# Modulated projections of a diffusion layer: half of the shifts added after the first eight outputs

## The chip, the cores and the metric

The kernel runs on one core of a Trainium2 chip. The core has five engines with a queue each: TensorE (PE; its weight loads are listed as PEld), VectorE (DVE), ScalarE (ACT), GpSimd (POOL) and SyncE (SP, here for transfers only). Sixteen DMA engines move data between the chip's memory (HBM), SBUF and back; PE writes to PSUM. The metric is device time in microseconds (us) of one execution, as the median of the runs shown.

## The reference

One layer over 512 latent tokens x of width 2048, with 256 context tokens ctx. A condition vector c modulates the latent tokens, another, c_ctx, the context tokens. Cut to what the change touches:

```python
sc_ = silu(c); scc = silu(c_ctx)
mod_x = sc_ @ w_ada + b_ada            # w_ada: 2048 x (6 * 2048)
mod_c = scc @ w_ada + b_ada
sh1, s1, g1, sh2, s2, g2 = split(mod_x, 6); sh1c, s1c = first two of mod_c
h  = rmsnorm(x,   norm1_w) * (1 + s1)  + sh1
hc = rmsnorm(ctx, norm1_w) * (1 + s1c) + sh1c
p, pc = h @ w_in, hc @ w_in            # queries, keys, values of 8 heads; low-rank cq (384), ckv (256); k_rope (64)
# keys and queries get a rotary embedding (latent tokens alone), cq and ckv an RMSNorm
```

Differential attention and latent attention over context and latent tokens, the output projection and a gated MLP with a convolution follow; the change leaves them as they are. All numbers are float32. Since h is a sum of a scaled token and a shift that is the same for every token, h @ w_in is the scaled tokens' product plus one number for each output feature, shift @ w_in.

## The kernel before

**Layout.** Tokens lie along the free axis and features on the 128 partitions, in 16 tiles kt of 128 features. A projection's *feature* is a block of 128 output features; its weights come as two blocks of 512 KB (eight kt each, `wblock`, L87 and L90), and it is a sum over 16 kt. Every float32 factor is split into a high part (rounded by ACT, `wh`, `a2k`, `c2k`) and a low part (what is left, a subtraction on DVE, L81), and a product is three matmuls (`mm3`, L104 to L106): high by high, high by low, low by high. With 512 latent and 256 context tokens a feature is 96 matmuls. `a2k` tiles hold latent tokens (512 wide), `c2k` two context tiles of 256.

**The modulation.** c and c_ctx are loaded as rows, go through SiLU on ACT and are spread over 128 partitions by PE (L199), into `cb` and `ccb`. A modulation number is a dot product of 2048 terms. `scales(u)` makes the scales of the pair kt = 2u, 2u + 1 on PE: four loads of 512 KB (`adak`, four buffers), 32 narrow matmuls with c and c_ctx in two of 32 columns (`cpad`, L219), a copy, two matmuls with `sel` that add up four partial sums (L223), and `a1` on DVE (L235). `shifts(kt)` makes the shift: two halves of 512 KB on SP's queue (L244), and for even kt two custom sums on DVE a half (L251, one for c and one for c_ctx, 1024 wide); for odd kt 16 PE transposes (L258) and 32 narrow matmuls. The later modulations (second shift and scale, gate; 48 blocks of 1 MB) are `gemv`s: a load (L168, SP's queue, two buffers) and one custom sum on DVE (L171).

**The stages.** First, squares of the tokens on ACT (L276, L277), their sums over features on PE with a matrix of ones (L282, L284), and the reciprocal root (L157). Then for kt from 0 to 15: the modulation of the next pair, the scaled and shifted tokens (`h` on DVE, L330, high part on ACT, L332, low part on DVE, L333), and nine outputs at once in PSUM: five features of the latent tokens (two of ckv, the keys of heads 0 and 1, the query of head 0) and four of the context. After these come seven single features with context (keys of heads 2 to 7 and k_rope), with three `gemv`s each; three of cq with two each; V in two halves of eight blocks, with one or two `gemv`s a block; then the heads, whose scores are L482.

**What sets the order.** Each engine works its queue in order. The program is written as one sequence; a scheduler that reckons with costs of its own spreads it over the engines' queues ahead of the run, and puts instructions under `high_priority` early. A transfer whose buffer is not free waits at the head of its queue, and what stands behind it in the queue waits too. `reuse_waits="tile"` makes a pool's next user wait for the same tile's last reader alone. Only the MLP's end is written in an order by hand.

Of the kernel before, what the change touches and what calls it, by code (L numbers as in the profile page):

```python
# [9 lines left out]
F32 = mybir.dt.float32  # L10
# [7 lines left out]
P = 128  # L18
# [34 lines left out]
def layer_kernel(ctx: ExitStack, tc: tile.TileContext, small, rope, c_row, cc_row, x_t, ctx_t, ada, ada_k,  # L53
# [33 lines left out]
    def wblock(src, cols=1024, pool=None):  # L87
        pool, full = (pool, cols) if pool else (wp, 1024)
        raw = pool.tile([P, full], F32, tag="wr", name=nm("wr"), bufs=3 if full == 1024 else 2)
        nc.sync.dma_start(raw[:, :cols], src)  # L90
        hi = pool.tile([P, full], F32R, tag="wh", name=nm("wh"), bufs=3)
        lo = pool.tile([P, full], F32R, tag="wl", name=nm("wl"), bufs=3)
        split(hi[:, :cols], lo[:, :cols], raw[:, :cols])
        return hi, lo
# [15 lines left out]
    sm.tile([P, 88], F32, name="edge")  # L110
# [69 lines left out]
    hcp = tc.alloc_tile_pool(name="hcp", bufs=17, side="right")  # L180
# [3 lines left out]

    st = tc.alloc_tile_pool(name="st", bufs=1, reuse_waits="tile")

    cb = st.tile([P, D], F32, name="cb")
    ccb = st.tile([P, D], F32, name="ccb")  # L190
# [3 lines left out]
    for row, wide in ((c_row, cb), (cc_row, ccb)):  # L194
        nc.sync.dma_start(wide[0:1], row)
        sc.activation(wide[0:1], wide[0:1], AF.Silu)
        for j in range(0, D, 512):
            t = b_tile()
            pe.matmul(t, ones32[0:1], wide[0:1, j:j + 512], start=True, stop=True)  # L199
            ve.tensor_copy(wide[:, j:j + 512], t)  # L200
    exp_ln_tables()

# [6 lines left out]

    g0b = [b_tile() for _ in range(4)]  # L210
    acc = g0b[3]

    def products(src, n):


        for j in range(4):
            for c in range(4):
                kt = 4 * j + c
                pe.matmul(acc[32 * c:32 * c + 32, :n], cpad[:, kt], src(kt), start=j == 0, stop=j == 3)  # L219
        row = st.tile([P, 2 * P], F32, tag="row", name=nm("row"), bufs=1)[:, :n]  # L220
        sc.copy(row, acc[:, :n])
        for i in range(n // P):
            pe.matmul(acc[:, 2 * i:2 * i + 2], row[:, i * P:(i + 1) * P], sel, start=True, stop=True)  # L223

    def scales(u):

        ws = []
        for j in range(4):
            wk = st.tile([P, 4, 2 * P], F32, tag="adak", name=nm("adak"), bufs=4)
            nc.sync.dma_start(wk, ada_k[u, j // 2][:, (j % 2) * 4:(j % 2) * 4 + 4])  # L230
            ws.append(wk)
        products(lambda kt: ws[kt // 4][:, kt % 4], 2 * P)
        for i in range(2):
            kt = 2 * u + i
            ve.tensor_scalar(out=a1[:, 2 * kt:2 * kt + 2], in0=acc[:, 2 * i:2 * i + 2], scalar1=b1[:, kt:kt + 1],  # L235
                             scalar2=col("n1", kt), op0=ALU.add, op1=ALU.mult)

    def shifts(kt):


        ws = []
        for hf in range(2):
            w = st.tile([P, D // 2], F32, tag="ada", name=nm("ada"), bufs=5)
            nc.sync.dma_start(w, ada[kt][:, hf * D // 2:(hf + 1) * D // 2])  # L244
            ws.append(w)
        dst = [m[:, kt:kt + 1] for m in (modx, modc)]
        if kt % 2 == 0:
            for hf, w in enumerate(ws):
                for i, (vec, d) in enumerate(zip((cb, ccb), dst)):
# [5 lines left out]
        for q in range(4):  # L255
            for i in range(4):
                k = (q % 2) * 4 + i
                pe.transpose(acc[:, i * P:(i + 1) * P], ws[q // 2][:, k * P:(k + 1) * P], ident)  # L258
# [1015 lines left out]
```

## Time and profile before

| | |
|---|---|
| median of 3 runs (lowest, highest) | 2450.04 us (2447.59, 2454.52) |
| profiled execution | 2454.1 us, span 2451.9 us, mean granted clock 0.988 |
| PE busy | 2375.5 us, 97% of the span |
| DVE, ACT, POOL busy | 1726.3, 1102.5, 242.1 us |
| moved by DMA | 403.31 MB, mean 164 GB/s |
| queue of SP and ACT, queue of POOL | 350.87 MB, 49.30 MB |

The page's slices cut the span into 40 equal parts of 61.3 us; a digit is the busy share in tenths. A stretch of a table by stage has its length, the busy time and number of instructions of each engine, the clock that was granted to PE, the DMA share and GB/s. A group is a line of the program, engine, operation, output and inputs, shapes, the number of instructions, then the busy time, the mean ns of one, and the idle time of the engine ahead of them with what ended it. In the chain of waits each row is a start, a length, and the work or wait that held up what came after.

### The profile page before, as it was taken

Reading aid. Unit: us, or ns where it says so; the run is one execution under the profiler, and the core shown is the slowest. Engines: PE = TensorE matmul, PEld = TensorE weight load, DVE = VectorE, ACT = ScalarE, POOL = GpSimd, SP = SyncE. Lnnn points to the kernel's source line nnn. Section 1 sums busy time; section 2 is a strip of 40 time slices with the busy share of each in tenths; the row PEclk is TensorE's granted clock in tenths of the full one; section 3 lists DMA queues with packets and bytes.
Section 4 is the critical chain, followed back from the end, with each engine's and each line's share of the span. In section 5 each row is a group of like instructions: output and inputs, shape, how many; then the busy total and the mean of one; then the engine's idle time right before and its main releaser. Section 6 shows DMA issues by size and latency. Waiting matters only on the chain.

```text
span 2451.9 us, 32940 instructions
## 1 busy us (share of the span) xinstructions
PE 2375.5 (97%) x12788; PEld 1988.9 (81%) x12788; DVE 1726.3 (70%) x2272; ACT 1102.5 (45%) x1666; POOL 242.1 (10%) x270
## 2 busy tenths in 40 slices
PE   7999999999999999999999999999999999999997
PEld 3778887877777778888888888888888888888887
DVE  4668785388868877377666666666666666666667
ACT  4342121155545542244545454545454545454553
POOL 0000000122100003100111111111111111111113
PEclk8999999999999999999999999999999999999999
DMA  7868898554411149423555655555555555555572
GB/s 276 283 228 297 321 340 289 189 181 137 141 59 44 44 159 337 152 85 112 134 141 135 141 135 141 134 142 134 140 135 143 133 143 133 144 132 142 133 213 78
DMA packets 130706, 403.31 MB, mean 164 GB/s; under 512 B 14323, under 2 KB 25075, under 8 KB 122099
## 3 DMA queue, kind: packets, MB, share of 16 engines
q1 hardware_dynamic: 104118, 350.87, 43.4%
q0 software_dynamic: 25280, 49.30, 11.5%
q8 instruction: 100, 1.64, 0.3%
q10 hardware_dynamic: 1152, 1.05, 0.1%
q14 instruction: 56, 0.46, 0.1%
HBM read 331.68 MB, written 69.48 MB: 164 GB/s over the span
## 4 chain that ended last, share of the span: by engine, by line
PE 84%; DVE 8%; ACT 3%; DMA 3%; issue 1%; POOL 1%; SPq 0%; DVEq 0%; ACTq 0%; POOLq 0%
PE y L973 12%; PE b L105 10%; PE b L104 10%; PE b L106 10%; PE z L973 6%; PE y L975 6%; PE z L975 3%; PE s L104 3%; PE s L105 3%; PE s L106 3%; PE s L482 3%; PE x L973 2%; DMA ada<-in_ada 2%; PE x L975 1%; PE f L104 1%
## 5 line engine op out<-in xcount | busy, mean ns | idle before, releaser
L104 PE MATMUL b<-ah,wh 128*128 128x512 f32 (+1 forms) x672 | 259.1, 386 | 0.0
L105 PE MATMUL b<-al,wh 128*128 128x512 f32 (+1 forms) x672 | 259.0, 385 | 0.0
L106 PE MATMUL b<-ah,wl 128*128 128x512 f32 (+1 forms) x672 | 258.0, 384 | 0.0
L994 POOL DMA_DIRECT2D x_d<-xs x160 | 139.7, 1003 | 1166.4 <-ACT xs L993 1164.3
L949 DVE TENSOR_TENSOR wl<-wr,wh 128x1024 fp32r<-128x1024 f32 x126 | 153.8, 1221 | 128.7 <-ACT wh L943 128.7
L949 DVE TENSOR_TENSOR wl<-rb,wh 128x1024 fp32r<-128x1024 f32 x124 | 151.2, 1220 | 128.0 <-ACT wh L943 128.0
L80 ACT CAST wh<-wr 128x1024 fp32r<-128x1024 f32 (+3 forms) x118 | 115.9, 982 | 259.0 <-PE b L105 68.3
L943 ACT CAST wh<-wr 128x1024 fp32r<-128x1024 f32 x126 | 132.3, 1050 | 206.3 <-PE b L105 100.7
L943 ACT CAST wh<-rb 128x1024 fp32r<-128x1024 f32 x124 | 130.2, 1051 | 190.0 <-PE b L105 112.5
L949 DVE TENSOR_TENSOR wl<-ws,wh 128x1024 fp32r<-128x1024 f32 x123 | 150.1, 1221 | 88.8 <-ACT wh L943 88.8
L81 DVE TENSOR_TENSOR wl<-wr,wh 128x1024 fp32r<-128x1024 f32 (+3 forms) x118 | 137.3, 1164 | 89.4 <-ACT wh L80 89.0
L171 DVE CUSTOM_DVE_ANT_0 ada<-ada,cb,smt 128x2048 f32<-128x2048 f32 x64 | 151.6, 2369 | 62.4 <-DMA ada<-in_ada 62.1
L943 ACT CAST wh<-ws 128x1024 fp32r<-128x1024 f32 x123 | 128.3, 1043 | 137.0 <-PE b L105 45.2
L106 PEld LDWEIGHTS b<-ah,wl 128*128 128x128 f32 x672 | 126.3, 188 | 25.6
L104 PEld LDWEIGHTS b<-ah,wh 128*128 128x128 f32 x672 | 126.6, 188 | 22.9
L105 PEld LDWEIGHTS b<-al,wh 128*128 128x128 f32 x672 | 126.6, 188 | 22.0
L104 PE MATMUL b<-a2k,wh 128*128 128x512 f32 (+1 forms) x352 | 133.1, 380 | 6.6 <-ACT a2k L756 5.0
L106 PE MATMUL b<-a2k,wl 128*128 128x512 f32 (+1 forms) x352 | 132.5, 376 | 0.0
L973 PE MATMUL y<-b2k,wh 128*128 128x512 f32 x410 | 106.9, 390 | 0.0
L484 DVE TENSOR_REDUCE m<-s 128x1 f32<-128x768 f32 x96 | 90.5, 949 | 15.3 <-PE s L482 14.9
L993 ACT ACTIVATE xs<-b,modx 128x512 f32<-128x512 f32 x160 | 101.0, 680 | 0.5 <-PE y L973 0.3
L973 PEld LDWEIGHTS y<-b2k,wh 128*128 128x128 f32 x410 | 77.0, 188 | 17.1
(471 smaller groups left out, 5937.4 us busy)
## 6 DMA issues: line engine op xcount, KB each, us to landing
ada<-in_ada SPq DMA_DIRECT2D x64, 1024.0 KB, 6.8
rb<-in_w_up SPq DMA_DIRECT2D x123, 512.0 KB, 4.4
wr<-in_w_dn SPq DMA_DIRECT2D x84, 512.0 KB, 4.3
x_d<-xs POOLq DMA_DIRECT2D x160, 256.0 KB, 6.0
wr<-in_w_up SPq DMA_DIRECT2D x53, 512.0 KB, 4.2
wr<-in_w_f SPq DMA_DIRECT2D x34, 512.0 KB, 5.9
adak<-in_ada_k SPq DMA_DIRECT2D x32, 512.0 KB, 6.2
ada<-in_ada SPq DMA_DIRECT2D x32, 512.0 KB, 6.6
```

The costliest lines, as they stand in the source:

```text
L80: sc.copy(dst_h, src)
L81: ve.tensor_tensor(dst_l, src, dst_h.bitcast(F32), op=ALU.subtract)
L104: pe.matmul(out, st[0], mv[0], start=start, stop=False, **kw)
L105: pe.matmul(out, st[0], mv[1], start=False, stop=False, **kw)
L106: pe.matmul(out, st[1], mv[0], start=False, stop=stop, **kw)
L171: ve.tensor_tensor_reduce(out=junk, in0=w, in1=vec, op0=ALU.mult, op1=ALU.add, scale=1.0, scalar=col("b_ada", j), accum_out=dst[:, j:j + 1])
L943: sc.copy(hi, raw)
L949: ve.tensor_tensor(lo, raw, hi.bitcast(F32), op=ALU.subtract)
L973: pe.matmul(o, w[j][0], hs[j], start=start and j == 0, stop=False, skip_group_check=True)
L975: pe.matmul(o[:, h0], w[j][1], hs[j][:, h0], start=False, stop=j == 7, skip_group_check=True)
L993: sc.mul(x, po, modx[:, 80 + dt:81 + dt])
L994: gp.dma_start(x1_d[dt], x, accum_op=ALU.add)
```

## The change

- Tokens are loaded first. The condition rows come later, spread over 128 partitions by the load itself (1 MB each), and SiLU runs on all partitions; PE's broadcast is gone. `cb` stays in place for the whole projection part.
- All 16 shifts are sums on DVE, with halves loaded on POOL's queue, three buffers. PE's transposes and narrow matmuls for odd kt are gone. Three halves are issued ahead of a copy on POOL that waits for `ccb`.
- While the nine first outputs are made, only the shifts of kt 8 to 15 are computed and applied. kt 0 to 7 go in scaled but unshifted. The outputs are copied as they are, and kept (`keep`).
- The next three features (`EARLY`) are projected from the same half-shifted tokens and kept too, while shifts 0 to 7 are computed. Then `add_shift` puts these into the tokens: high and low part are added, shifted, and split again. The fourth feature takes its second half of kt first.
- `biases` makes what is missing from the eight outputs: the eight blocks of the first outputs and three first half blocks of weights are loaded again, raw, through the two raw buffers of the ring, and multiplied by the shifts in 40 narrow matmuls. `with_bias` adds it to the kept outputs, and their keys, query and norms are made after features 3, 4 and 5.
- `gemv`s: none with feature 3, two with 4 to 6, three with each of cq, three or two with V's blocks. Rings: raw weight blocks have two buffers instead of three up to the end of V; `adak` six instead of four.

```diff
-    for row, wide in ((c_row, cb), (cc_row, ccb)):
-        nc.sync.dma_start(wide[0:1], row)
-        sc.activation(wide[0:1], wide[0:1], AF.Silu)
-        for j in range(0, D, 512):
-            t = b_tile()
-            pe.matmul(t, ones32[0:1], wide[0:1, j:j + 512], start=True, stop=True)
-            ve.tensor_copy(wide[:, j:j + 512], t)
...
+        for hf in range(2):
+            w = sp_.tile([P, D // 2], F32, tag="ada", name=nm("ada"), bufs=3)
+            gp.dma_start(w, ada[kt][:, hf * D // 2:(hf + 1) * D // 2])
+            for i, (vec, d) in enumerate(zip((cb, ccb), dst)):
+                t = w if i else sp_.tile([P, D // 2], BF16, tag="junk", name=nm("junk"), bufs=1)
+                ve.tensor_tensor_reduce(out=t, in0=w, in1=vec[:, hf * D // 2:(hf + 1) * D // 2], op0=ALU.mult,
+                                        op1=ALU.add, scale=1.0, scalar=d if hf else col("b_ada", kt), accum_out=d)
...
     modulation(0)
+    for row, wide in ((c_row, cb), (cc_row, ccb)):
+        nc.sync.dma_start(wide, row.to_broadcast([P, D]))
+        sc.activation(wide, wide, AF.Silu)
+    gate = sm.tile([P, 1], F32, name="gate")
+    gp.tensor_copy(gate, ccb[:, 0:1])
...
     for kt in range(KT):
-        if kt % 2 == 0 and kt < KT - 2:
-            modulation(kt // 2 + 1)
+        if kt % 2 == 0:
+            if kt < KT - 2:
+                modulation(kt // 2 + 1)
+            shifts(KA + kt // 2)
...
+                if kt < KA:
+                    split(*hl, t)
+                else:
+                    shifted(*hl, t, m[:, kt:kt + 1])
...
+    def add_shift(kt):
+        for i, (hl, m, n_) in enumerate(((hx[kt], modx, T), (hc[kt], modc, C))):
+            t = rtmp()[:, :n_]
+            ve.tensor_tensor(t, hl[0].bitcast(F32), hl[1].bitcast(F32), op=ALU.add)
+            shifted(*hl, t, m[:, kt:kt + 1])
...
+        for kt in range(KA):
+            w = wraw(w_g0[kt], 640)
+            r = slice(32 * (kt % 4), 32 * (kt % 4) + 32)
+            pe.matmul(ac[0][r], spad[:, kt], w[:, :512], start=kt < 4, stop=kt >= KA - 4)
+            pe.matmul(ac[1][r, :P], spad[:, kt], w[:, 512:640], start=kt < 4, stop=kt >= KA - 4, skip_group_check=True)
+        for e in range(EARLY):
+            w = wraw(w_f[feats[e], 0])
...
+    for e in range(EARLY):
         lat, co = b_tile(), s_tile()
         feature(lat, co[:, :C])
+        for kt in (range(3), range(3, 6), range(6, 8))[e]:
+            shifts(kt)
+        keep(5 + e, lat, co[:, :C])
+    for kt in range(KA):
+        add_shift(kt)
+    sp_.release()
+    gvp = tc.alloc_tile_pool(name="gvp", bufs=1, side="right", reuse_waits="tile")
+    for f in range(EARLY, 7):
+        lat, co = b_tile(), s_tile()
+        feature(lat, co[:, :C], halves.get(f, (0, 1)))
         keys(k_d[f + 2] if f < 6 else kr_d, lat, co[:, :C])
-        next_gemv(kv, 3)
+        if f == EARLY:
+            biases()
...
+        next_gemv(gvp, 2 if f > EARLY else 0)
```

Three places show how the queues change. The first is DVE's queue ahead of the second pair's scales (`a_91`). Before, the shift of kt 1 came from PE, two short additions (L262) stood there, with the low parts of the first tokens:

```order
L262 TENSOR_SCALAR modx<-b_189,smt 128x1
L262 TENSOR_SCALAR modc<-b_189,smt 128x1
L333 SCALAR_TENSOR_TENSOR a2k_567<-h_568,modx,a2k_566 128x512
L333 SCALAR_TENSOR_TENSOR c2k_529<-h_568,modc,c2k_528 128x256
L235 TENSOR_SCALAR a_91<-b_189,b_92,smt 128x2 x2
L330 SCALAR_TENSOR_TENSOR h_704<-a2k_205,a_91,rinv 128x512
```

Now ten sums of shift halves (L248) stand there, of which the last six are these (each is followed by an entry of one column that writes the sum):

```order
L248 ISA ada_532,modc<-ada_532,ccb,smt 128x1024
L248 ISA modc 128x1
L248 ISA junk_539,modx<-ada_537,cb,modx 128x1024
L248 ISA modx 128x1
L248 ISA ada_537,modc<-ada_537,ccb,modc 128x1024
L248 ISA modc 128x1
L248 ISA junk_660,modx<-ada_658,cb,smt 128x1024
L248 ISA modx 128x1
L248 ISA ada_658,modc<-ada_658,ccb,smt 128x1024
L248 ISA modc 128x1
L237 TENSOR_SCALAR a_91<-b_220,b_92,smt 128x2 x2
L321 SCALAR_TENSOR_TENSOR h_546<-a2k_175,a_91,rinv 128x512
```

So the second pair's scales, which PE's sums give, are behind shift sums of later tiles that read `cb` and `ccb`.

The second place is DVE's queue in the middle of `add_shift`, which the program before doesn't have (L444 adds the parts, L303 makes the new low part, L174 is a `gemv`, L81 a weight block's low part):

```order
L444 TENSOR_TENSOR rt_1799<-a2k_544,a2k_545 128x512
L444 TENSOR_TENSOR rt_1803<-c2k_542,c2k_543 128x256
L174 ISA ada_2276,modx<-ada_2276,cb,smt 128x2048
L174 ISA modx 128x1
L81 TENSOR_TENSOR wl_1757<-wr_1754,wh_1756 128x1024
L303 SCALAR_TENSOR_TENSOR a2k_545<-rt_1799,modx,a2k_544 128x512
L303 SCALAR_TENSOR_TENSOR c2k_543<-rt_1803,modc,c2k_542 128x256
L444 TENSOR_TENSOR rt_1807<-a2k_580,a2k_581 128x512
L444 TENSOR_TENSOR rt_1811<-c2k_542,c2k_543 128x256
L174 ISA ada_2279,modx<-ada_2279,cb,smt 128x2048
```

Four `gemv`s and three low parts of weights stand among the additions ahead of the last one.

The third place is SP's queue at the raw blocks of `biases`. Before, a feature's blocks and the `gemv` loads alternated in twos:

```order
L389 DMA k_d_130<-kl_1929 128x768
L90 DMA wr_2043<-in_w_f 128x1024
L90 DMA wr_2049<-in_w_f 128x1024
L168 DMA ada_2069<-in_ada 128x2048
L168 DMA ada_2072<-in_ada 128x2048
L90 DMA wr_2176<-in_w_f 128x1024
L90 DMA wr_2182<-in_w_f 128x1024
```

Now:

```order
L89 DMA wr_1989<-in_w_g 128x640
L89 DMA wr_1993<-in_w_g 128x640
L171 DMA ada_2713<-in_ada 128x2048
L89 DMA wr_1997<-in_w_g 128x640
L89 DMA wr_2001<-in_w_g 128x640
L171 DMA ada_2716<-in_ada 128x2048
L89 DMA wr_2005<-in_w_g 128x640
L89 DMA wr_2009<-in_w_g 128x640
L171 DMA ada_2719<-in_ada 128x2048
L89 DMA wr_2013<-in_w_f 128x1024
L89 DMA wr_2023<-in_w_f 128x1024
```

Raw blocks, in twos, and 1 MB loads of `gemv`s stand in turns in one queue.

More of the change, by code (lines that the diff above doesn't have):

```diff
@@ L225, in scales @@
[L225 to L236, printed above, removed]
```

214 lines of the change are left out of this document (127 added, 87 removed).

## The prediction

> **What bounds the kernel now.** I read the page's slices first, then the chain of waits up to 620 us, then busy time by stage, and last the groups of instructions inside the stages that the change touches. Times are us from the span's start.
>
> ```profile
> PE   7999999999999999999999999999999999999997
> DVE  4668785388868877377666666666666666666667
> ```
>
> TensorE is nine tenths busy in every slice except the first and the last, so only time in which it idles, or works on something that can go, is to be had. The chain says what that is at the start:
>
> ```profile
> 7.16 14.02 PE b L199 x16
> 26.55 1.57 PE s L282 x4
> 28.83 1.57 PE s L282 x4
> 39.49 1.30 PE s L284 x4
> 47.62 1.54 DVE h L330 x3
> 52.37 1.22 PE s L104 x2
> 364.13 7.53 DMA ada<-in_ada
> 374.07 7.40 DMA ada<-in_ada
> ```
>
> The condition vector is broadcast for 14 us before the sums of squares can run (2.28 us for two token tiles), and the first projection matmul comes at 52.37. Far later, the V projection waits for the 1 MB loads of the modulation: one buffer of the two comes round every 9.9 us.
>
> ```profile
> 52.00:186.00 134.00, 129.34 (x1076) 98.68 (x1076) 89.72 (x174) 50.86 (x99) 0.00 (x0) 0.97 0.73 249
> 186.00:270.00 84.00, 83.26 (x470) 72.15 (x471) 70.61 (x98) 22.13 (x29) 0.00 (x0) 1.00 0.85 308
> 270.00:344.00 74.00, 74.00 (x369) 61.64 (x368) 60.49 (x67) 18.02 (x24) 0.00 (x0) 1.00 0.90 338
> 344.00:411.00 67.00, 66.40 (x293) 54.38 (x291) 46.34 (x47) 11.82 (x14) 0.00 (x0) 1.00 0.84 303
> 411.00:481.00 70.00, 66.02 (x279) 54.40 (x280) 30.09 (x30) 12.27 (x15) 2.63 (x4) 0.95 0.60 202
> 496.00:2452.00 1956.00, 1911.44 (x10165) 1624.37 (x10164) 1400.55 (x1811) 958.36 (x1437) 231.11 (x251) 0.99 0.50 136
> ```
>
> (Columns: stretch, length, busy PE, PEld, DVE, ACT, POOL, clock, DMA share, GB/s.) These are the first nine outputs (52 to 186), five single features (to 270), the other five (to 344), V (to 481) and everything after the scores begin (from 496), which the change leaves alone. What the reader is to see: from 186 to 344 VectorE is busy 83% and DMA moves 308 to 338 GB/s while PE is full. Three resources are nearly level there, so PE time saved earlier is kept only if VectorE and DMA have room to follow.
>
> **The change part by part.** Prices on PE first:
>
> ```profile
> 200.00:220.00 20.00, 20.00 (x117) 1.00 0.89 323
> L258 PE MATMUL b<-ident,ada 128*128 128x128 f32 x112 | 17.7, 280 | 1.4 <-ACT wt L259 1.4
> L219 PE MATMUL b<-adak,cpad 128*32 128x256 f32 x224 | 14.4, 384 | 0.0
> ```
>
> 117 matmuls in 20 us, half of 512 and half of 256 columns, are 0.445 ns a column. One token tile of the first nine outputs has 10,752 columns (4.8 us; sixteen 77 us); a feature with context 36,864 (16.4 us). The scales of a pair are 32 matmuls, 1.9 us with 0.6 for the sums behind them: 2.5 us.
>
> *Start.* The 14 us of broadcast go, and the tokens no longer wait for it.
>
> ```profile
> L276 ACT ACTIVATE sq<-a2k 128x512 f32<-128x512 f32 x15 | 9.3, 622 | 13.8 <-PE s L282 8.9 <-DVE sqs L279 4.9
> L277 ACT ACTIVATE sq<-c2k 128x256 f32<-128x256 f32 x15 | 6.0, 399 | 0.0
> L196 ACT ACTIVATE cb<-cb 1x2048 f32<-1x2048 f32 x1 | 1.9, 1892 | 0.0
> ```
>
> A first square at about 5.5, then eight pairs at 2.28, ends near 24. From the last sum (39.49) to the scaled tokens (47.62) before were 8 us, of which 1.8 were shifts that now aren't waited for; with a multiply and a cast (0.74 each) the first projection comes at about 33, 19 us early. Bounds: 30, if no square waits for its tokens; 37, if the 24 token tiles of 256 KB and the three shift halves beside them (7.9 MB) come at the 308 GB/s of the second stage above.
>
> *First features.* All odd shifts leave PE: (134 − 77 − 7 × 2.5) / 8 = 5 us each, 40 in all. Against that one new wait. VectorE's queue holds ten pieces of shift sums ahead of the second pair's scales, and these need the broadcast vectors, whose SiLU runs on ACT (2 × 1.9 us and a table load) behind two 1 MB loads: first piece at 39 to 40, ten pieces of 1.28 done at 53, the second pair's multiplies behind them, PE again at 57. The first pair's work on PE ends at 33 + 2.5 + 9.6 + 2 = 47: PE idles 10. First features end at 33 + 77 + 17 + 10 = 137, against 186.7. This is the largest gain in the kernel, and the next part says how little of it stays.
>
> *Shifts 0 to 7 and their addition.* VectorE's prices:
>
> ```profile
> L81 DVE TENSOR_TENSOR wl<-wr,wh 128x640 fp32r<-128x640 f32 x14 | 11.5, 820 | 0.1
> L333 DVE SCALAR_TENSOR_TENSOR a2k<-h,modx,a2k 128x512 fp32r<-128x512 f32 x15 | 11.2, 750 | 5.8 <-ACT a2k L332 5.8
> L330 DVE SCALAR_TENSOR_TENSOR h<-a2k,a,rinv 128x512 f32<-128x512 f32 x14 | 9.8, 744 | 0.0
> L251 DVE CUSTOM_DVE_ANT_0 ada<-ada,ccb,modc 128x1024 f32<-128x1024 f32 x7 | 9.0, 1284 | 0.2
> L333 DVE SCALAR_TENSOR_TENSOR c2k<-h,modc,c2k 128x256 fp32r<-128x256 f32 x15 | 7.2, 479 | 0.0
> ```
> ```profile
> L171 DVE CUSTOM_DVE_ANT_0 ada<-ada,cb,smt 128x2048 f32<-128x2048 f32 x48 | 112.8, 2349 | 50.5 <-DMA ada<-in_ada 50.2
> L81 DVE TENSOR_TENSOR wl<-wr,wh 128x1024 fp32r<-128x1024 f32 x38 | 46.4, 1221 | 26.9 <-ACT wh L80 26.7
> L81 DVE TENSOR_TENSOR kl<-rt,kh 128x512 fp32r<-128x512 f32 x9 | 6.2, 687 | 0.7 <-ACT kh L80 0.6
> ```
>
> From 57 VectorE owes seven token pairs at 2 × (0.74 + 0.48 + 0.75 + 0.48 + 0.82) + 0.3 = 6.8 (48 us), 54 pieces at 1.28 (69), and 7 weight splits at 1.22 (9): it is done at 183. The eight additions follow, each two sums (0.69 as the split of a key below, and 0.44 for half the columns, by the ratio of the lower halves) and two lower halves (0.75 and 0.48): 2.36, together 19. Four 1 MB products (9.4) and three or four splits (4.3) stand among them, and the first product's load starts only when the shifts' pool is released (+3). The last shifted tile exists at about 218 to 219. PE meanwhile has done features 0 to 2 (137 + 49 = 186) and half of feature 3 (194), then follows tile by tile and ends feature 3 at 219 instead of 202: **17 us given back**. Since VectorE sets 219, the 10 us stall and the start have that much cover: if this cover were gone (a faster VectorE), they would cost their 10 us. Before, feature 3 ended at 187 + 4 × 16.7 = 253; the lead is 34 now.
>
> *The bias matrix.* Eleven raw blocks (eight of 320 KB, three of 512 KB) pass through two buffers, with 40 narrow matmuls among those of the next feature (4.5 us with the two sums). Each pair of loads is issued when the pair before has been multiplied. The nearest rows:
>
> ```profile
> adak<-in_ada_k SPq DMA_DIRECT2D x24, 512.0 KB, 6.3
> wr<-in_w_g SPq DMA_DIRECT2D x12, 320.0 KB, 5.9
> ```
> ```profile
> DMA packets 10792, 51.24 MB, mean 320 GB/s; under 512 B 1188, under 2 KB 1188, under 8 KB 7069
> ada<-in_ada SPq DMA_DIRECT2D x30, 1024.0 KB, 6.7
> wr<-in_w_f SPq DMA_DIRECT2D x18, 512.0 KB, 7.3
> ```
>
> After the first pair five rounds of 5.9 to 7.3 are 30 to 37 us, 21 of them beside the feature's and the bias's own work on PE. The next feature's blocks queue behind them in the same ring. I take 38 us for this feature (rounds of 6.5, and 5 for its beginning and end): over at 257, not 240, 17 lost. Lower bound: nothing lost, if the loads land early; upper bound: 17 to 20 more, if every round waits behind a 1 MB load (9.9). Before, this point was at 270: lead 13.
>
> *To V.* Two features and three query blocks are 68 us of PE; VectorE owes ten products (23.5), ten splits (12), and the keys, norms and first queries: five keys of five rope and split operations at 0.69 and one of 0.44 (3.9 us each, 20), the rest at the same prices some 18: 74 to 80. V begins at 331 to 337 (344 before). The lead is 7 to 13.
>
> *V.* 33 of the 48 products are left for V, 21 before. 33 MB of them and 8 MB of weights at 303 to 320 GB/s are 128 to 135 us, by the buffers' round (9.9 for two) up to 142 within the 14 blocks that they fill, against PE's 132 (16 × 8.25). V took 137 before; I take 142, end at 473 to 479 against 481. The first scores also wait for V rows written by POOL, where before for PE alone: between nothing and a landing of 6 us, and I take 2, since the last of six is half covered by the projections ahead. Net: 0 to 6 earlier, and I take 2.
>
> Against the profiled execution (span 2451.9, 2454.1 by the clock) that is 2452; the runs' median lies 4 us below the profiled one, so the forecast is **2448**.
>
> One row on the clock belongs here, since the change makes three idle stretches of over 5 us:
>
> ```profile
> 414.98 0.76 PE L104 MATMUL s<-wh,a2k 128*128 128x512 f32 x1 [4.58 <-DVE kl L81]
> ```
> ```profile
> 415.00:416.00 1.00, 1.00 (x3) 0.50 1.35 268
> 420.00:421.00 1.00, 1.00 (x5) 0.56 1.00 280
> 421.00:422.00 1.00, 1.00 (x6) 1.00 1.04 255
> ```
>
> After 4.6 us without work the granted clock was 0.50 until about 420.6: 5.6 us at half speed cost 2.8. I put nothing into the sum for it, since the stall at 47 lies under VectorE's ledger and those in the bias feature under its loads; without that cover three stalls are 8 us. The Trainium skill ("TensorE: Matmul & The Clock Gate", Part 1: The HAM clock gate) says the clock halves after an idle window of about 3.4 us and returns after about 3.4 us of sustained work; that would be 1.7 us a stall, an estimate, against 2.8 by the trace, and I go by the trace.
>
> **The rivals.** *B, the waits overlap.* If bias loads land early and VectorE never idles, V's start is set by VectorE's work alone: the first pair and ten pieces 21, then the 126 to the last shift, the additions with what stands among them 33, three keys and four splits 17, and the 74 to 80, from 33 on: 304 to 310. With some 14 us of waits left it is 322; with 140 for V and 2 for the scores the end is 464, 17 early: **2433**. For it: 338 GB/s was reached from 270 to 344. Against: VectorE's 50 us of waiting for loads in the row above, in a stage with fewer bytes.
>
> *C, slower: the bias loads stand behind 1 MB loads.* One queue, SP's, carries both in order; a product's load is issued only when a buffer is free, and what stands behind it waits too. If rounds take 9.9 instead of 5.9 to 6.5, some 20 us are lost with no cover left: **2468**. It decides from a round of about 7, where the 2 us of the net are gone. For it: in the changed order three 1 MB loads stand between the bias blocks. Against: no trace shows this mixture.
>
> *D, the shifts come late.* Their loads go through POOL and three buffers. The only transfers of POOL in this part of the kernel are writes of V:
>
> ```profile
> 487.27 0.75 POOL L470 DMA_DIRECT2D v_d<-kh  x1 [1.52 <-ACT kh L80]
> ```
>
> A round is 0.75 for the issue, 6.3 for landing and 2.6 for the sums: 9.7 us for three halves, worth 7.7 of VectorE. Where VectorE has nothing else to do it idles 2 in 9.7; for the sixteen halves beside features 0 to 2 that is up to 10 us on the path: **2458**. For it: 512 KB landings of 6.3 above. Against: splits and token work fill gaps. The Trainium skill ("SBUF — State Buffer", Who interferes with whom) says descriptors written by GpSimd stall only beside VectorE's two-port modes, not beside an operation with two inputs; no run here shows it, and by it D would stay at the buffers' round.
>
> **How the numbers follow.** Forecast 0.40, B 0.28, C 0.18, D 0.14. About 0.3% (7.4 us, 2442.7 to 2457.4) is what a measurement can tell from no change. The forecast has an own range of 2440 to 2457: 0.05 of its 0.40 is faster, 0.02 slower, and 0.33 the same. B is faster but for 0.01. C is slower but for 0.02. D is half same. Faster 0.05 + 0.27 = 0.32, same 0.33 + 0.01 + 0.02 + 0.07 = 0.43, slower 0.02 + 0.16 + 0.07 = 0.25; the landings were all taken from stages in which DMA is fuller than it need be here, and I move 0.05 from same to faster and slower for that: 0.36, 0.38, 0.26. The range takes in B and C: 2429 to 2470.
>
> **What would show it.** First projection at 30 to 36; an idle PE near 47 to 57 that ends on VectorE; first single feature at 135 to 142; PE waiting in feature 3 for the additions, ended by ACT or VectorE, near 195 to 219; waits on raw blocks in the next; V's start at 331 to 337. The forecast is wrong if feature 3 runs without waits (B), if the bias feature takes over 45 us (C), or if VectorE waits for POOL's loads from 140 to 185 (D).

## The result, and the profile after

The changed kernel takes 2486.81 us (median of 4 runs, 2482.28 to 2496.39) against 2448.82 before: 1.0156 times as long, 95% interval 1.0121 to 1.0190. The forecast was 2448, no change, with 2429 to 2470 as its range: wrong, by some 39 us, on the side of the rivals C and D, and further out than either.

Its profiled execution has a span of 2483.7 us, 31.8 more than before (by the medians it is 38.0). The slices of the page that answer to the two shown of before:

```profile
PE   5999899899999889989999999999999999999997
DVE  4998886478877777458857576767676767676767
```

In the first slice TensorE has 5 for 7: the broadcast is gone from it. Then it has small holes: in the middle of the projections (the fifth slice, 248 to 310 us) and at their end (the eighth, 435 to 497), and, not to be expected from the diff, in slices 14, 15 and 18 (807 to 931 and 1056 to 1118). Where the 31.8 us arise can be read from one line of the program, the scores, which has first and last starts of each operand in its instructions (count, min/median/max ns, then from when to when). Before, and then after:

```profile
L482 PE MATMUL s<-ks,qs x128: 277/391/765, 495.2 to 678.3; 128*128 128x512 f32 x64, 128*128 128x256 f32 x64
L482 PE MATMUL s<-krlz,qs x64: 278/376/481, 711.0 to 867.6; 128*128 128x512 f32 x32, 128*128 128x256 f32 x32
```
```profile
L551 PE MATMUL s<-ks,qs x128: 274/377/504, 509.1 to 688.7; 128*128 128x512 f32 x64, 128*128 128x256 f32 x64
L551 PE MATMUL s<-krlz,qs x64: 278/388/632, 720.9 to 894.4; 128*128 128x512 f32 x32, 128*128 128x256 f32 x32
```

With the end of V's last matmul (480.2 before, 485.6 after, from the timeline) and the spans this gives:

| up to | before | after | later by | added here |
|---|---|---|---|---|
| last matmul of V | 480.2 | 485.6 | 5.4 | 5.4 |
| last score of the first attention | 678.3 | 688.7 | 10.4 | 5.0 |
| last score of the second attention | 867.6 | 894.4 | 26.8 | 16.4 |
| end | 2451.9 | 2483.7 | 31.8 | 5.0 |

Only 5.4 of 31.8 us come from the projections, which the change is about. 21.4 come from the stages behind the first attention, whose code it does not touch.

What differs in the second attention is on ScalarE. PE, DVE and POOL have the same instructions in the same order there in both kernels. ScalarE's groups (689 to 894 us) hold something that the kernel before has not at this place:

```profile
L162 ACT ACT_TABLE_LOAD x7 | 9.0, 1283 | 0.1
L163 ACT ACT_TABLE_LOAD x6 | 7.7, 1283 | 0.1
```

ACT_TABLE_LOAD loads the tables of a set of functions; the kernel's `exp_ln_tables` asks for the set with exponential and logarithm. L162 and L163 are the logarithm and the exponential of the reciprocal root (`rstd`). Over the whole execution these lines load a table 22 times, of 28 loads in all. Below them are all loads of the kernel before, four:

```profile
L162 ACT ACT_TABLE_LOAD x11 | 14.1, 1283 | 0.2
L163 ACT ACT_TABLE_LOAD x11 | 14.1, 1283 | 0.2
```
```profile
L155 ACT ACT_TABLE_LOAD x2 | 2.6, 1283 | 0.0
L193 ACT ACT_TABLE_LOAD x1 | 1.3, 1283 | 3.8 <-DMA smt<-in_small 3.8
L822 ACT ACT_TABLE_LOAD x1 | 1.3, 1283 | 0.0
```

The kernel before loads the set that holds both functions behind its SiLUs (L201, which calls L155), and then no table until the MLP. The changed kernel loads it ahead of `rstd`, at L266; the SiLUs of the condition vectors (L278) come later now and load a set of their own, and so does the exponential behind them (L291). From then on each logarithm and each exponential of an `rstd` loads a table, so neither finds its set in place.

What this does to PE shows in the stretch between the two last scores, before and after (columns as in the table by stage of before):

```profile
678.30:867.60 189.30, 179.84 (x976) 144.20 (x975) 146.83 (x257) 103.89 (x203) 3.44 (x4) 0.98 0.15 47
688.70:894.40 205.70, 186.65 (x976) 148.31 (x975) 147.03 (x256) 119.81 (x213) 3.44 (x4) 0.95 0.14 43
```

Of the 16.4 us, 9.6 are idle time of PE (19.1 us, 9.5 before). The other 6.8 are the same 976 matmuls taking longer, at a granted clock of 0.95 instead of 0.98.

The second find is at the end of V. A row of the timeline has a start, a length, the instruction, and in brackets the idle time of the engine ahead of it and what ended it. Before, and then after:

```profile
495.24 0.77 PE L482 MATMUL s<-ks,qs 128*128 128x512 f32 x1 [4.89 <-DMA ks<-k_d]
```
```profile
496.10 0.76 PE L107 MATMUL f<-a2k,wh 128*128 128x512 f32 x1 [10.55 <-DVE kl L81]
```

Before, the query projection of the next head (`f`) followed V without a gap, and PE then waited 4.89 us for the first keys. Now `f` waits 10.55 us for the copies out of V's own PSUM tiles. PSUM tiles are handed out in turn from four banks; the change uses 16 ahead of V where there were 22, so the second half of V lies in the two banks that `f` takes over. In the same way the keys of the first heads (`ks`) now lie in SBUF under the last tiles of V: the loads of the first wait 8.1 us on SP's queue for V's copies (`kl`), those of the second 2.4 us for a write of V.

The projections themselves, by stage (columns as in the table by stage of before):

```profile
63.00:148.00 85.00, 84.97 (x582) 66.62 (x583) 78.94 (x142) 27.24 (x49) 7.40 (x14) 0.97 0.80 276
148.00:200.00 52.00, 52.00 (x299) 45.52 (x298) 49.07 (x72) 15.19 (x26) 5.29 (x10) 1.00 0.70 238
200.00:221.00 21.00, 21.00 (x132) 18.86 (x131) 21.00 (x31) 7.62 (x13) 0.00 (x0) 1.00 0.64 211
221.00:264.00 43.00, 31.21 (x164) 19.59 (x162) 22.02 (x39) 7.29 (x13) 0.31 (x1) 0.75 0.82 298
264.00:333.00 69.00, 62.32 (x285) 50.20 (x286) 63.60 (x93) 26.56 (x38) 0.00 (x0) 0.91 0.85 309
```

These are the first outputs from the second pair on, features 0 to 2, feature 3 beside the additions, the feature with the bias matrix, and what follows. From 63 to 221 TensorE has no holes. From 221 to 264 it is busy for 31 of 43 us, and at a clock of 0.75.

### The profile page after: what moved, and what is told of

Read it like the earlier page. It is cut to its first block, busy times and chain, and to the rows that moved or that the text cites. A ratio compares the mean times of both kernels' runs of the same rounds, so it can differ in the third digit from the quotient of the medians.

```text
span 2483.7 us, 32417 instructions
## 1 busy us (share of the span) xinstructions
PE 2363.8 (95%) x12468; PEld 1979.4 (80%) x12468; DVE 1772.7 (71%) x2348; ACT 1135.2 (46%) x1694; POOL 258.6 (10%) x304
## 4 chain that ended last, share of the span: by engine, by line
PE 68%; issue 16%; DVE 8%; ACT 4%; DMA 2%; POOL 1%; SPq 0%; POOLq 0%; DVEq 0%; ACTq 0%
PE y L1042 12%; PE b L108 7%; PE b L107 7%; PE b L109 7%; PE z L1042 6%; PE y L1044 6%; PE z L1044 3%; PE x L1042 2%; PE s L551 2%; PE f L107 1%; PE x L1044 1%; PE s L107 1%; PE s L108 1%; PE s L109 1%; PE f L108 1%
## 5 line engine op out<-in xcount | busy, mean ns | idle before, releaser
L81 DVE TENSOR_TENSOR wl<-wr,wh 128x1024 fp32r<-128x1024 f32 (+3 forms) x118 | 136.6, 1161 | 84.2 <-ACT wh L80 75.9
L174 DVE CUSTOM_DVE_ANT_0 ada<-ada,cb,smt 128x2048 f32<-128x2048 f32 x64 | 151.4, 2368 | 60.2 <-DMA ada<-in_ada 60.2
L107 PEld LDWEIGHTS b<-a2k,wh 128*128 128x128 f32 x352 | 68.4, 195 | 33.8 <-ACT a2k L80 11.7
```

The lines of the kernel that those rows point to most:

```text
L81: ve.tensor_tensor(dst_l, src, dst_h.bitcast(F32), op=ALU.subtract)
L107: pe.matmul(out, st[0], mv[0], start=start, stop=False, **kw)
L174: ve.tensor_tensor_reduce(out=junk, in0=w, in1=vec, op0=ALU.mult, op1=ALU.add, scale=1.0, scalar=col("b_ada", j), accum_out=dst[:, j:j + 1])
```

## Experiments

**Two causes outside the projections.** The first four kernels test the two finds, the first also in the other direction, on the kernel before.

*The tables, mended.*

```diff
     for row, wide in ((c_row, cb), (cc_row, ccb)):
         nc.sync.dma_start(wide, row.to_broadcast([P, D]))
         sc.activation(wide, wide, AF.Silu)
+    exp_ln_tables()
```

> The changed kernel with the table of exponential and logarithm loaded again right behind the two SiLUs of the condition vectors; nothing else. Theory (tables): 22 table loads of 1.28 us ahead of each Ln and Exp go (the profile counts 28 loads, 6 stay); the stretch from the last score of the first attention to the last score of the second falls from 205 to about 189 us, and the time from 2487 to 2460 to 2466. Rival (order: the scheduler's other order of the latent attention is what costs): the stretch stays at 200 to 206 and the time within 5 of 2487.

Measured: 2463.57 us, 1.0059 times before (1.0039 to 1.0079): 23 us less than the changed kernel. The scores of the second attention and the tables of `rstd`'s lines:

```profile
L552 PE MATMUL s<-ks,qs x128: 274/389/562, 511.7 to 692.4; 128*128 128x512 f32 x64, 128*128 128x256 f32 x64
L552 PE MATMUL s<-krlz,qs x64: 278/376/477, 725.2 to 881.8; 128*128 128x512 f32 x32, 128*128 128x256 f32 x32
```

From the last score of the first attention to the last of the second 189.4 us now, 189.3 before, 205.7 in the changed kernel. Both lines of `rstd` have no table load left.

*The tables, lost in the kernel before.*

```diff
     gp.memset(cpad, 0.0)
+    exp_ln_tables()
...
             ve.tensor_copy(wide[:, j:j + 512], t)
-    exp_ln_tables()
```

> The kernel before with one line moved: the table of exponential and logarithm is loaded ahead of the SiLUs instead of behind them, so that each later Ln and Exp loads its own (28 loads instead of 4 to 6). Theory (tables): 2469 to 2477, the second attention 14 to 18 us longer. Rival (order): within 4 us of the kernel before.

Measured: 2473.06 us, 1.0097 times before (1.0079 to 1.0115): 22 us more, within what the theory expected. Here the loads come back, and the stretch is 205.9 us, though the other instructions are those of the kernel before, in an order that differs from it only up to 176 us:

```profile
L159 ACT ACT_TABLE_LOAD x12 | 15.4, 1283 | 0.2
L160 ACT ACT_TABLE_LOAD x12 | 15.4, 1283 | 0.2
```

With that the rival, another order of the second attention, is out. Thirteen of the loads (16.7 us of ScalarE) lengthen a stage of 189 us by 16.4, though ScalarE was busy for only 104 us of it before: they stand on the way from a norm to the scores that wait for it. That 16.4 us is near the length of the loads is chance: PE's idle time grew by 0.7 us a load, and the lower clock made the rest. The Trainium skill ("ScalarE: Activation LUTs", What ACT_TABLE_LOAD costs) gives 1283 ns for a load, as the rows do, and 2.66 us for a switch with its drain. Here a load cost about 1.3 us of the stage, the clock's part included, and about 1.1 of the whole (23 us for 22), so the measurement stays below the page. The Trainium skill ("ScalarE: Activation LUTs", Table sets: the hidden batching unit) says that one set holds exponential and logarithm, so that the one after the other needs no second load. The mended kernel agrees with that; the changed kernel, with two loads for each pair, does not, and the measurement decides: nothing behind its SiLUs asked for the set with both.

*The places, mended.* No work is left out.

```diff
     latent_norm(cq, T, QR, "qn", cq_d)
+    for _ in range(2):
+        ve.memset(b_tile()[:, 0:1], 0.0)
     for half in range(2):
...
     def da_head(h, qs):
+        if h == 0:
+            da.tile([P, TT], F32, tag="p0", name=nm("p0"), bufs=8)
```

> The changed kernel with two memory places moved and no work left out: two PSUM tiles are written with one column each ahead of V, so that the second half of V lies in other banks than the query projection behind it, and the keys of the first heads get SBUF that does not lie under the last V tiles. Theory (places): PE no longer idles 10.6 us at 485 and the first scores come at 495 to 500 instead of 509, time 2470 to 2477. Rival (eviction: the tail of V with its 12 writes is what the scores wait for, wherever they lie): first scores at 505 or later, time 2482 or more.

Measured: 2482.22 us, 1.0128 times before (1.0102 to 1.0155), some 4 to 5 us less than the changed kernel (1.0156), and the intervals overlap. The place is as the theory said: the idle of 10.55 us is gone and the first scores come at 493.8.

```profile
L553 PE MATMUL s<-ks,qs x128: 277/390/795, 493.8 to 680.3; 128*128 128x512 f32 x64, 128*128 128x256 f32 x64
```

But the first attention takes 186.5 us from there, not 179.6. In the changed kernel PE's wait stood ahead of `f`, and the keys landed while `f` ran; now `f` follows V at once, and PE waits behind it, as before the change:

```profile
493.81 0.76 PE L553 MATMUL s<-ks,qs 128*128 128x512 f32 x1 [4.31 <-issue]
```

The granted clock of the attention is 0.96 instead of 1.00. From V's last matmul to the last score it was 198.1 us before, 203.1 in the changed kernel, and it is 201.0 here (199.6 in the next kernel). The size expected, 10 to 17 us, was wrong: I had counted the shift of the first score, 13.9 us, of which only 5.0 arrive at the end of this attention.

*Both.* The edits of the first and the third kernel together.

> The changed kernel with both of the edits above. If both causes are right and lie one behind the other, they add: 2446 to 2456, level with the kernel before, and what is left of the difference is the end of V, 5 us later than before. If one hides the other, 2457 to 2470.

Measured: 2457.57 us, 1.0030 times before (1.0015 to 1.0045). It is 6 us below the one with tables alone. What remains is about 7 us (4 to 11 by the interval). The stages behind V take as long as before in its profile (1970.3 us against 1971.7), so it belongs to the projections. In its profile V ends at 491.2, later than in the other three profiles with the same projections (479.3 to 489.0): these stages vary by several us from one execution to the next.

**What the projections lose.** The next runs start from the kernel with both mended (2457.6).

*Without the bias matrix.* The raw blocks and matmuls are left out and `beta` is zero, so that the first eight outputs lack half of their shift.

```diff
     def biases():
-        spad = rtmp()[:, :KA * 32].rearrange("p (k i) -> p k i", i=32)
...
-            ve.tensor_copy(beta[:, 8 * n_:8 * n_ + 8], ac[n_][:, :8])
+        ve.memset(beta, 0.0)
```

> The kernel with tables and places mended, without the bias matrix: the eleven raw blocks are not loaded, the 48 narrow matmuls are left out and zeros are added instead, so that the first eight outputs lack half of their shift. Theory (the raw blocks' two buffers cost 20 us that nothing hides): the feature behind the additions takes 17 to 20 us instead of 41 to 46, V starts 18 to 24 earlier, at 322 to 334, and the time falls from 2457 to 2435 to 2442. Rival (VectorE's and DMA's work sets V anyway): the time stays within 7 of 2457.

Measured: 2433.05 us, 0.9929 times before (0.9902 to 0.9956). V's first matmul comes at 314.7 instead of 355.8 and its last at 452.1. The bias matrix costs about 24 us, and without it the kernel would be 0.7% faster than the one before.

*More buffers, and the products put off.* Five buffers for the raw blocks, in the memory that `gvp` uses, so the 1 MB products start only behind them.

```diff
+    bip = tc.alloc_tile_pool(name="bip", bufs=5, side="right", reuse_waits="tile")
-    gvp = tc.alloc_tile_pool(name="gvp", bufs=1, side="right", reuse_waits="tile")
...
-            w = wraw(w_g0[kt], 640)
+            w = braw(w_g0[kt], 640)
...
             biases()
+            bip.release()
+            gvp = tc.alloc_tile_pool(name="gvp", bufs=1, side="right", reuse_waits="tile")
```

> The kernel with tables and places mended; the eleven raw blocks get five buffers of their own, in the memory that the shifts leave, and the 1 MB products begin only when these are free again, so none stands among the additions or among the raw blocks. Theory (it is the two buffers and the queue): additions end 5 to 9 us earlier, the feature with the bias takes 22 to 28 us instead of 41 to 46, V starts 15 to 25 earlier; time 2440 to 2450. Rival (products put off pile up in V, which their loads already fill): V's start is earlier, its end is not, time 2454 or more.

Measured: 2474.32 us, 1.0093 times before (1.0067 to 1.0118): the rival was right. V begins at 338.9, but PE then waits in it:

```profile
436.08 0.77 PE L107 MATMUL s<-wh,a2k 128*128 128x512 f32 x1 [14.07 <-DVE kl L81]
454.44 1.22 PE L107 MATMUL s<-wh,a2k 128*128 128x512 f32 x2 [10.18 <-ACT wh L80]
```

*More buffers, products where they were.* The four buffers in which keys are split serve the raw blocks.

```diff
+    def braw(src, cols, i):
+        raw = kvs.tile([P, TT], F32, tag=("kh", "kl")[i % 2], name=nm("bw"))
+        nc.sync.dma_start(raw[:, :cols], src)
+        return raw
...
-            w = wraw(w_g0[kt], 640)
+            w = braw(w_g0[kt], 640, kt)
...
-            w = wraw(w_f[feats[e], 0])
+            ws = [braw(w_f[feats[e], 0][:, h * 512:(h + 1) * 512], 512, h) for h in range(2)]
```

> The kernel with tables and places mended; the raw blocks of the bias matrix use the four buffers of 3 KB in which keys are split, instead of the two of the weights' ring (the last three blocks as halves). Nothing is left out and no product is put off. Theory (two buffers, each free only when PE has used it, make the raw blocks come at a landing's pace): the feature with the bias takes 25 to 32 us instead of 41 to 46, V starts 8 to 18 earlier than the 348 to 356 of the kernels with two, time 2440 to 2450. Rival (the bytes cost it, 4 MB at 300 GB/s and the clock): V starts at 344 or later, time within 6 of 2457.

Measured: 2462.77 us, 1.0055 times before (1.0039 to 1.0070): no gain. Its stretches, and below them the same ones of the kernel with two buffers:

```profile
222.00:264.00 42.00, 41.60 (x252) 27.88 (x251) 20.69 (x38) 12.32 (x21) 0.31 (x1) 1.00 0.72 253
264.00:300.00 36.00, 28.13 (x132) 23.01 (x131) 33.43 (x53) 10.23 (x18) 0.00 (x0) 0.90 0.82 295
400.00:490.00 90.00, 77.39 (x328) 62.19 (x327) 55.44 (x53) 15.21 (x18) 1.32 (x2) 0.94 0.82 282
```
```profile
222.00:264.00 42.00, 29.65 (x143) 18.10 (x145) 18.93 (x35) 5.67 (x11) 0.31 (x1) 0.80 0.74 267
264.00:300.00 36.00, 32.10 (x174) 26.82 (x167) 30.27 (x48) 13.39 (x21) 0.00 (x0) 0.80 0.81 284
400.00:490.00 90.00, 87.64 (x380) 72.07 (x379) 53.52 (x50) 14.65 (x18) 0.56 (x1) 0.98 0.77 273
```

The holes in the bias feature are gone (41.6 of 42 us busy, the clock at 1.00), and V starts at 341.6 instead of 355.8: the landmarks of the theory, but the time of the rival. The same time is lost again in V: it takes 149 us instead of 135, with 12.7 us of idle PE instead of 2.4. The raw blocks also take buffers from the keys here; what that costs by itself was not tried.

*Loads without matmuls, and matmuls without loads.* The first loads the eleven blocks and multiplies nothing (`beta` is zero); the second makes all narrow matmuls from one block of each kind, so the bias is that of wrong weights.

```diff
         for kt in range(KA):
-            w = wraw(w_g0[kt], 640)
-            r = slice(32 * (kt % 4), 32 * (kt % 4) + 32)
...
+            wraw(w_g0[kt], 640)
+        for e in range(EARLY):
+            wraw(w_f[feats[e], 0])
+        ve.memset(beta, 0.0)
```

> The kernel with tables and places mended; the eleven raw blocks are loaded through their two buffers and nothing reads them: the narrow matmuls are left out and zeros are added as the bias. Theory (transfers bind: 3.9 MB more at about 320 GB/s are 12 us ahead of the products' loads): 2443 to 2450, 10 to 17 above the 2433 without loads and matmuls. Rival (it is PE that holds the buffers): 2430 to 2438.

```diff
-            w = wraw(w_g0[kt], 640)
+            if kt == 0:
+                w = wraw(w_g0[kt], 640)
...
-            w = wraw(w_f[feats[e], 0])
+            if e == 0:
+                w = wraw(w_f[feats[e], 0])
```

> The same base with all 48 narrow matmuls, but only one block of the first outputs and one of the later features loaded for them, so that the bias is made from the wrong weights. Theory (transfers bind): 2436 to 2443, the 5 us of the narrow matmuls and their sums above the 2433. Rival (PE's narrow matmuls and the half clock behind them cost it): 2450 or more.

Measured: 2442.24 us with loads alone (0.9966 times before, 0.9947 to 0.9985), 2436.43 with matmuls alone (0.9934, 0.9908 to 0.9960). By the medians the loads alone cost about 9 us, a little under the 10 to 17 that I expected, the matmuls alone about 3, and both 24, so that about 12 would arise only where they meet. The intervals are 4 to 7 us to either side: the 9 is just clear of nothing, the 3 is not, and the 12 is rough. A raw block is loaded when PE has used the one two places ahead, and PE waits for its landing. That the 12 lie in these waits is not shown: with four buffers they were gone, and the time was no shorter.

The bytes by the end of V, before (to 480) and after (to 486):

```profile
DMA packets 38926, 133.18 MB, mean 277 GB/s; under 512 B 3811, under 2 KB 9955, under 8 KB 32622
```
```profile
DMA packets 40704, 138.56 MB, mean 285 GB/s; under 512 B 4012, under 2 KB 10156, under 8 KB 34274
```

5.4 MB more are 17 to 19 us at 285 to 320 GB/s, a part of which the higher rate takes back.

What the products of 1 MB have to do with it can be read from VectorE's rows in the timeline (how many of the 48 had begun, and when the last did) and from PE's in V:

| kernel | begun at 240 | 320 | 400 | last one | V's first and last matmul | PE idle in V |
|---|---|---|---|---|---|---|
| before | 7 | 23 | 39 | 446.6 | 339.2, 480.2 | 4.6 |
| changed | 10 | 20 | 34 | 464.4 | 348.4, 485.6 | 4.1 |
| both mended | 9 | 19 | 33 | 469.0 | 355.8, 491.2 | 2.4 |
| without bias | 9 | 22 | 39 | 435.8 | 314.7, 452.1 | 2.7 |
| four buffers | 8 | 17 | 32 | 473.3 | 341.6, 490.5 | 12.7 |
| five buffers, products put off | 0 | 10 | 27 | 491.8 | 338.9, 506.2 | 25.9 |

From 320 on each kernel gets through about 8 to 9 products in 40 us. The change has begun 10 at 240, three ahead, and has lost three by 320: this is where the raw blocks, the keys of the kept outputs and the fewer products of each feature stand. V's weights stand behind the products' loads in SP's queue. But in the first four kernels PE is idle for 2.4 to 4.6 us of V only, so that V's end follows from its start and from PE's own work; the changed kernel's V is late because it begins late. Only in the last two does PE wait long: 8.0 us for weights with four buffers, and with five 10.2 us for weights and 14.1 for copies of V's first half, whose writes stand in the same queue. There what V's start won is lost again. So the products are a second limit, not far behind PE. The number of products left does not tell by itself when it binds: 21 had begun at V's start without bias, and 20 with four buffers. No run changed the products' pace alone.

**The start alone.** On the kernel before.

```diff
-    for row, wide in ((c_row, cb), (cc_row, ccb)):
-        nc.sync.dma_start(wide[0:1], row)
...
+    xs, cs = [], []
+    for kt in range(KT):
+        xt = a2k()
+        nc.sync.dma_start(xt, x_t[kt])
...
+    exp_ln_tables()
     rstd(rinv, ssq[:, :TT], D, sqs, nt2)
     g0w = []
 
+    def vectors():
+        for row, wide in ((c_row, cb), (cc_row, ccb)):
+            nc.sync.dma_start(wide, row.to_broadcast([P, D]))
+            sc.activation(wide, wide, AF.Silu)
+        exp_ln_tables()
...
         for kt in (2 * u, 2 * u + 1):
+            if u == 0 and kt == 0:
+                vectors()
             shifts(kt)
```

> The kernel before with only the start of the change: tokens loaded first, condition vectors spread by the load, SiLU on all partitions, tables loaded behind it; shifts as before. Theory (the first shift needs the spread vectors, so the start alone gives little): first projection at 46 to 50 instead of 52.4, time 2444 to 2451. Rival (the 14 us of broadcast go as a whole): first projection at 40, time 2436 to 2441.

Measured: 2441.04 us, 0.9956 times before (0.9943 to 0.9970). The rival was right again: the 14 us of broadcast go nearly as a whole. The chain of its start:

```profile
34.57 1.54 DVE h L333 x3
36.11 1.20 DVE junk L252
38.75 1.20 DVE junk L252
40.77 1.22 PE s L104 x2
```

The first shift (`junk`) is taken right behind the token's scaling; the vectors are there in time, and the first projection comes at 40.8, 11.6 us earlier than before. It stays so: V starts at 331.3 (339.2) and ends at 471.0 (480.2), and the end is 8.2 us earlier in the profiles. This kernel, with one part of the change, is faster than both the kernel before and the changed one.

## Why the prediction was wrong

**The step that failed is a phrase at the start of the prediction: "everything after the scores begin (from 496), which the change leaves alone".** It put 0 where the profiles show 21.4 us, 16.4 in the second attention and 5.0 behind it, and mending the tables took 23 us from the time. The reason was in the diff: the line that loads the tables now stands ahead of two SiLUs that stood ahead of it before. I read its place as the start's affair and wrote "a table load" into the start's sum, without asking which set is left in place for the rest of the program. The profiles show 28 loads after and 4 before. With tables and places mended the kernel takes 2457.6 us, inside the range that was given: the rest of the sum was off by less.

**The second step is "The first scores also wait for V rows written by POOL ... I take 2".** A wait came at this place, and it cost 5.0 us at the end of the attention, but by another mechanism: the query projection waited 10.55 us for V's copies out of its own banks, and the key loads for the memory under V's last tiles. POOL wrote the rows in the mended kernel too, where that idle time is gone. What I hadn't seen is that PSUM banks are handed out in turn, so that the number of tiles ahead of V decides what the next projection waits for.

**The projections: the form right in the main, the sum 7 to 13 us short.** V's end was forecast at 473 to 479 and came at 485.6.

- *Start:* forecast 33, came 39.3. The first square was put at 5.5 and ran at 5.1, but those behind it waited for their tokens, the last time for a context tile until 13.1. Three 512 KB loads of POOL's queue went out beside them; in the kernel with the start alone, which has none there, each token load on record landed 3.2 to 5.6 us after its issue.

```profile
3.06 10.00 DMA c2k<-in_ctx_t
13.09 0.42 ACT sq L256
31.47 1.30 PE s L263 x4
45.67 1.28 DVE junk L248
```

The last sums came at 31.5, not 24; from there the 8 us held. The bound of 37 was too low by 2. In the other profiled kernels that begin like this one the first projection came between 39.4 and 49.6: one execution tells little about this point.
- *The new wait ahead of the second pair:* forecast 10 us, ended at 57. It was 7.95 and ended at 63.0, and the first piece of a shift came at 45.7, not 39 to 40, behind the late start. The first outputs ended at about 148, not 137.

```profile
62.99 0.79 PE L107 MATMUL b<-a2k,wh 128*128 128x512 f32 x1 [7.95 <-ACT a2k L80]
```
- *The additions:* forecast the last shifted tile at 218 to 219 and the end of feature 3 at 219; the tile came at 216.2 and the feature's end at 223.1. VectorE was busy for all of 200 to 221, as the ledger said. The 17 us of waiting in feature 3 did not show, because PE came to it 14 us late. So the sign that was set for B, feature 3 without waits, came true without B.

```profile
215.68 0.47 DVE L303 SCALAR_TENSOR_TENSOR c2k<-rt,modc,c2k 128x256 fp32r<-128x256 f32 x1
```
- *The bias matrix:* forecast 38 us with rounds of 6.5, over at 257. It took 41 from 223 to 264. SP's queue shows the rounds, pairs of raw blocks issued at 237.5, 245.3 and 249.8, and its waits (us in total, times, the longest) say what held them:

```profile
SPq L89 <- PE b L460: 15.5, 6, 4.7
SPq L89 <- DMA wr<-in_w_f: 5.5, 4, 2.2
SPq L171 <- DVE modx L174: 1.2, 1, 1.2
```

So it was mostly PE's use of the two buffers, and not the 1 MB loads of rival C, which waited 1.2 us once. C's time, 2468, was nearest to the result among the rivals, by a mechanism that did not occur.
- *To V:* 74 to 80 forecast from there, 84 measured (264.2 to 348.4). My landmark for V's start before, 344, was late too: its first matmul is at 339.2. So the lead of 7 to 13 us was in truth a lag of 9. PE's share, given as 68 us, is 65.6 at the prediction's own price of 0.445 ns a column; it set nothing, since VectorE's was longer.
- *V:* forecast 142, since 33 of the 48 products were to be left for it. It took 137: 24 had begun when it started, so 24 were left, and PE was idle for 4.1 us of it.

**The other rivals.** B (all waits overlap, 2433) did not happen. The kernel without the bias matrix ran in 2433 as well, but that is luck: it has tables and places mended and leaves work out, where B counted all work. D (shifts late by POOL's queue) did not happen: from 57 to 223 VectorE waited 5.8 us in all for shift halves, whose median landing from 60 to 185 was 4.9 us against the 6.3 that I took. The rule of the Trainium skill ("SBUF — State Buffer", Who interferes with whom), that an operation of VectorE with two inputs doesn't hold up the descriptors that GpSimd writes, agrees with these rows.

```profile
ada<-in_ada POOLq DMA_DIRECT2D x25, 512.0 KB, 4.9
```

**The clock.** I put nothing into the sum for it. In the bias feature it was 0.75, and with four buffers 1.00, with no gain at the end. In the second attention it was a cost: 6.8 of the 16.4 us. The stretch at half clock that the prediction read as 5.6 us is nearer 5.9, since the row from 420 to 421 still has 0.56; that is 2.9 us for 2.8.

**What stays open.** The mended kernel is 7 us slower than before, clear of noise over its eight runs (1.0015 to 1.0045), but single executions of the projections vary by more (V's end 479 to 491 in four profiles), so no row of one profile says where in them the 7 us lie. What four buffers won in the bias feature was lost again in V, where PE waited for weights; a kernel that changes nothing but the products' order was not run.

## What to carry to other kernels

A change at the start of a kernel can set a state that all later stages use: which activation tables are in place, and which bank or buffer comes next in turn. Compare the whole order of each queue, counting table loads, and not only the places that were edited. The table loads left TensorE idle more often here, and its granted clock fell (0.95 for 0.98), so they cost more than the idle time. And where a later stage has a limit of transfers close behind that of TensorE, time won on TensorE ahead of it is kept only as far as those transfers start earlier too.

## What was not expected of the hardware

- Thirteen table loads of 1.28 us on ScalarE, which was busy for little more than half of the stage, cost the stage 16.4 us: 9.6 of idle PE, and 6.8 by a granted clock of 0.95 instead of 0.98.
- With 11 raw blocks the loads alone cost about 9 us, the matmuls alone about 3, and both 24, with intervals of 4 to 7 us to either side.
- Three 512 KB loads of POOL's queue beside the tokens' first loads held these up: the second context tile took 10.0 us from its issue, and no token more than 5.6 in the kernel without them.
